# A hybrid decoder step: later weight parts, uncoupled sample scores, more output buffers, and the sample's output inside the last prompt tile

## The chip, the cores and the metric

The kernel runs on one core of a Trainium2 chip. Its engines are TensorE (PE, matrix products, with PEld for the loading of the stationary operand), VectorE (DVE), ScalarE (ACT), GpSimd (POOL) and SyncE (SP, which here issues every DMA). The metric is the device time of one execution in microseconds (us). Three runs of the kernel before gave 1445.16, 1446.93 and 1440.16 us; the median is 1445.16.

## The reference

One inference step of a one-layer decoder: a prompt of 2048 rows and a sample of 8 sequences with 8 new rows each, model width 1024.

```python
h = rmsnorm(x, norm_w)
z = h @ w_in      # q, k, v (512 each), qb, kb (256 each), vb (512), g_lr (16), gate_a, gate_b (512 each)
q = rope(rmsnorm(heads(q, 8), q_norm_w), pos); k = rope(rmsnorm(heads(k, 8), k_norm_w), pos)
o_a = attend(q, k, v)        # mixture of windows (128, step 1), (512, step 4), (2048, step 16)
log_a = log_sigmoid(g_lr @ w_gate_up + b_gate) / 16
o_b, s_fin = gla_chunked(qb / 8, kb, vb, log_a, s0)      # gated linear attention, 4 heads
o_b = rmsnorm(o_b, gla_norm_w)
y = x + concat(o_a * silu(gate_a), o_b * silu(gate_b)) @ w_out
```

The prompt attends within itself. The sample attends to caches of 2048 keys and values per sequence, and its linear attention starts from a given state. All is float32 at the interface; results are y for both, the new keys and values, and the states.

## The kernel before

**Arithmetic and tiles.** The prompt is cut into 16 tiles of 128 rows. A large product is made of three float16 products: an operand is scaled and split into a high and a low part, and high x high, high x low and low x high are summed in PSUM. The weights are cut into blocks of columns (q, k, v, qkb, g, vb, gb and the two halves of the output matrix). `load_w` loads one block as 8 raw tiles, finds its largest magnitude (squares on ACT, for v a reduction on DVE, then `spread_max` on PE), and makes the high and low parts on ACT and DVE. It is a generator: each `yield` lets other work be written in between, and `at_once` runs it to its end. The raw tiles have 8 buffers.

**Prompt rows.** `fetch(t)` loads x of tile t, into one buffer from tile 4 on. `prep(t)` normalises it, splits it, turns it by a transposing DMA (L499) and stores it for later blocks. `project(name, [t])` multiplies tile t by a block (L1056) and `post` takes the result out of PSUM.

**Attention of the prompt.** `attend` (L395 to L450) gives an item four stages: loads; scores on PE (L408), a mask and running minimum on DVE (L416) and exponentials on ACT (L419); transposes of the weights (L426) and their split (L388 to L393, where every second item uses ACT twice and POOL); the product with the values (L441). `pipeline` runs three items staggered by a stage. `unit` serves branches 1 and 2 (64 units, outputs in tile `o` of pool `op`, 4 buffers, stored at L843). `branch3(r)` serves the third branch for residue r of 16: it loads turned queries and keys (L881, L883), copies halves of the queries (`swapped`, L790, L791), loads values (L887), and stores its output tile `o3` (2 buffers of pool `b3`) at L900. The mask instruction writes into the output tile too, so it needs a free one.

**Scores of the sample.** `sample_scores(b, t)` (64 steps, L930 to L946) loads one query row broadcast to all partitions (L935) and cached keys (L937, L940), multiplies on POOL into the single buffer `pr` (L925) and sums on DVE (L926), twice per step. Steps are taken between projections from the third group of tiles on (`dot_next`), and the rest beside block qkb (`dots`).

**Stages.** First v, q, k of tiles 0 to 3; then v, q, k of tiles 4 to 15, with branches 1 and 2 of the tiles before; then block qkb and branch 3; then g, vb and gb with the linear attention; last the output products (`finish`, Y at L1422). Beside these runs the sample's attention, in 4 pairs of sequences: scores, softmax, and 26 value tiles of 8 buffers (`sv`, L1697) multiplied on PE (`OS`, L1671). Each pair ends with DVE's sum `soo` (L1711, L1712), which is stored and read again by `sample_out`, which makes the sample's own rows of y (Y_s).

**Order.** `weave` interleaves generators: always the one with the smallest (steps done + 0.5) / n goes next, so a part with a larger n is served more often. For the last stage the parts are the prompt's output with n = 286 and the sample's attention with n = 64. This gives the order in which instructions are written. The program is built with `schedule_with_timeline_sim=True`: the order on each engine is decided when the program is built, by a planned time at which operands and buffers are ready, and the written order says which goes first. So an instruction can stand far ahead of its place in the text.

## Time and profile before

| quantity | value |
|---|---|
| runs, median (lowest to highest) | 1445.16 us (1440.16 to 1446.93) |
| profiled execution | 1444.89 us |
| its span, first to last instruction | 1443.1 us |
| mean granted TensorE clock | 0.961 |
| PE busy | 89% |
| DVE busy | 70% |
| ACT busy | 59% |
| POOL busy | 43% |
| DMA engines, mean share on the main queue | 67% |

Busy shares are of the span. A line of a timeline gives start, duration, engine, line, operation, output<-input and count, and in brackets how long the engine was idle before it and what ended that. A line of waits gives engine, line and what it waited for, then us in total, times, and the longest. A line of a stretch gives its bounds and length, then busy us of PE, PEld, DVE, ACT and POOL with the number of instructions, the granted clock, the DMA share and GB/s. A line of a source gives minimum/median/maximum duration in ns and the first and last start.

### The profile page before, as it was taken

Reading aid. Unit: us, or ns where it says so; the run is one execution under the profiler, and the core shown is the slowest. Engines: PE = TensorE matmul, PEld = TensorE weight load, DVE = VectorE, ACT = ScalarE, POOL = GpSimd, SP = SyncE. Lnnn points to the kernel's source line nnn. Section 1 sums busy time; section 2 is a strip of 40 time slices with the busy share of each in tenths; the row PEclk is TensorE's granted clock in tenths of the full one; section 3 lists DMA queues with packets and bytes.
Section 4 is the critical chain, followed back from the end, with each engine's and each line's share of the span. In section 5 each row is a group of like instructions: output and inputs, shape, how many; then the busy total and the mean of one; then the engine's idle time right before and its main releaser. Section 6 shows DMA issues by size and latency. Waiting matters only on the chain.

```text
span 1443.1 us, 26500 instructions
## 1 busy us (share of the span) xinstructions
PE 1287.7 (89%) x8878; PEld 741.6 (51%) x8878; DVE 1013.1 (70%) x2445; ACT 853.1 (59%) x2295; POOL 624.8 (43%) x564
## 2 busy tenths in 40 slices
PE   4797998998989799997799999989889979999997
PEld 1343554555546455565466755667545435444343
DVE  6486877888798967667765446899978698773222
ACT  6635677677558866767667764778777543221120
POOL 0052334466667545664420376655752364340000
PEclk9998998999999999999799999999999999999998
DMA  9857585477866798879876453343225769988661
GB/s 280 253 163 181 149 215 145 125 204 224 207 181 190 171 271 260 281 231 245 233 186 161 137 169 103 101 133 119 71 103 192 258 203 339 377 286 267 227 205 62
DMA packets 255194, 285.36 MB, mean 198 GB/s; under 512 B 126209, under 2 KB 157010, under 8 KB 255058
## 3 DMA queue, kind: packets, MB, share of 16 engines
q1 hardware_dynamic: 255058, 283.67, 67.0%
q8 instruction: 70, 1.15, 0.3%
q14 instruction: 66, 0.54, 0.1%
HBM read 183.19 MB, written 75.24 MB: 179 GB/s over the span
## 4 chain that ended last, share of the span: by engine, by line
PE 35%; DVE 22%; DMA 19%; ACT 10%; issue 8%; POOL 4%; SPq 2%; DVEq 0%; POOLq 0%; ACTq 0%
PE Y L1422 8%; DMA T_q<-qp_d 3%; PE acc_vb L1056 3%; PE acc_g L1056 3%; PE OS L1671 3%; DMA x<-in_x_prompt 2%; PE s L408 2%; PE acc_q L1056 2%; PE acc_qkb L1056 2%; DVE p L416 2%; PE acc_v L1056 2%; DVE qbd L221 2%; PE t L426 2%; PE acc_k L1056 2%; ACT p L419 2%
## 5 line engine op out<-in xcount | busy, mean ns | idle before, releaser
L925 POOL TENSOR_TENSOR pr<-k,qb 128x512 f32<-128x512 f32 x128 | 174.8, 1366 | 188.7 <-DVE sck L926 111.7
L1056 PEld LDWEIGHTS <-hr 128*128 128x128 f16 x1824 | 177.6, 100 | 137.7 <-issue 16.5
L419 ACT ACTIVATE p<-p,o 128x256 f32<-128x256 f32 (+1 forms) x384 | 173.2, 453 | 84.3 <-DVE o L416 72.5
L1056 PEld LDWEIGHTS <-hl 128*128 128x128 f16 x1248 | 124.9, 102 | 157.5 <-issue 39.4
L1422 PE MATMUL Y<-w_o,mh 128*128 128x512 f16 x768 | 183.6, 387 | 10.4 <-ACT mh L1388 6.0
L416 DVE CUSTOM_DVE_ANT_0 p<-s,m3w,scl_s 128x256 f32<-128x256 f32 (+1 forms) x384 | 143.4, 418 | 34.4 <-DMA o_d<-o 20.8
L393 POOL TENSOR_TENSOR pt<-p,pt 128x512 f16<-128x512 f32 (+1 forms) x80 | 92.9, 1162 | 139.6 <-ACT pt L392 90.5
L441 PE MATMUL O<-v,pt 128*128 128x128 f16 x1200 | 115.6, 223 | 27.0 <-POOL pt L393 11.4
L426 PE MATMUL t<-ident,p 128*128 128x128 f32 x600 | 117.8, 286 | 14.3 <-ACT p L419 13.2
L1422 PEld LDWEIGHTS <-mh 128*128 128x128 f16 x768 | 72.8, 99 | 106.2 <-issue 27.1
L926 DVE TENSOR_REDUCE sck<-pr 128x8 f32<-128x512 f32 x128 | 87.1, 680 | 56.3 <-POOL pr L925 55.8
L408 PE MATMUL s<-kk,qq 128*128 128x256 f16 (+1 forms) x512 | 107.6, 324 | 17.5 <-DVE o L416 12.6
L1056 PE MATMUL acc_v<-w_v,hl 128*128 128x512 f16 x384 | 101.1, 410 | 13.0 <-ACT zs_k L648 4.6
L441 PEld LDWEIGHTS <-pt 128*128 128x128 f16 x1200 | 85.6, 100 | 51.8 <-POOL pt L393 15.7
L1056 PE MATMUL acc_g<-w_g,hr 128*128 128x272 f16 (+1 forms) x768 | 105.6, 288 | 5.3 <-DVE za L775 3.9
L1056 PE MATMUL acc_q<-w_q,hl 128*128 128x512 f16 x384 | 96.2, 394 | 2.1 <-ACT zs_q L648 1.4
L1056 PE MATMUL acc_k<-w_k,hl 128*128 128x512 f16 x384 | 92.9, 385 | 2.7 <-ACT zs_k L648 2.7
L1388 ACT ACTIVATE mh<-tm 128x1024 f16<-128x1024 f16 x32 | 31.7, 1020 | 104.1 <-PE tm L1387 97.7
L1056 PE MATMUL acc_vb<-w_vb,hr 128*128 128x512 f16 x384 | 91.4, 381 | 1.9 <-DVE so_g L622 1.9
L426 PEld LDWEIGHTS t<-ident,p 128*128 128x128 f32 x600 | 72.0, 145 | 36.0 <-ACT p L419 23.7
L1056 PE MATMUL acc_gb<-w_gb,hr 128*128 128x512 f16 x384 | 88.6, 384 | 0.1
L210 ACT ACTIVATE E<-D_e 128x256 f32<-128x256 f32 (+1 forms) x168 | 67.6, 412 | 31.7 <-DVE ks L217 21.2
(527 smaller groups left out, 2640.2 us busy)
## 6 DMA issues: line engine op xcount, KB each, us to landing
k<-in_cache_k_win SPq DMA_DIRECT2D x104, 256.0 KB, 4.4
sv<-in_cache_v_win SPq DMA_DIRECT2D x104, 256.0 KB, 5.5
hr<-h_d SPq DMA_DIRECT2D x44, 512.0 KB, 4.5
qb<-q_d SPq DMA_DIRECT2D x64, 256.0 KB, 4.7
oc<-o_d SPq DMA_DIRECT2D x48, 264.0 KB, 5.7
o_d<-o SPq DMA_DIRECT2D x64, 132.0 KB, 3.4
x<-in_x_prompt SPq DMA_DIRECT2D x16, 512.0 KB, 5.2
h_d<-hl SPq DMA_DIRECT2D x16, 512.0 KB, 5.1
```

The source lines that it names most:

```text
L210: ACT.activation(E[rows, i, :n], D[rows, half], AF.Exp, scale=1.0 / 16.0)
L393: POOL.tensor_tensor(l, f, h, ALU.subtract)
L408: PE.matmul(s_ps[:, i * w : (i + 1) * w], q, k, start=(n == 0), stop=(n == len(prods) - 1),)
L416: DVE.tensor_tensor_reduce(s[:, sl], s_ps[:, sl], mask, neg, BIG, ALU.add, ALU.min, nmf(i))
L419: ACT.activation(s[:, sl], s[:, sl], AF.Exp, bias=nmf(i), scale=-1.0, accum_out=denf(i))
L426: PE.transpose(p_ps[:, i * P : (i + 1) * P], t["s"][:, i * P : (i + 1) * P], ident[:])
L441: PE.matmul(o_, t["pt"][:, c, (i * nb + b) * P : (i * nb + b + 1) * P], vf(i, b), start=(n == 0), stop=(n == 2 * nb - 1),)
L925: POOL.tensor_tensor(pr[:], kt, qt, ALU.mult)
L926: DVE.tensor_reduce(out, pr[:].rearrange("p (u k d) -> p u k d", u=2, k=4), AX.X, ALU.add)
L1056: PE.matmul(z, a_[:, k, :], w[:, p_, k, cols], start=(k == 0 and i == 0), stop=(k == KT - 1 and i == 2),)
L1422: PE.matmul(Y[:], a_[:, k, :], w_[:, part, k, :512], start=(i == 0), stop=(i == len(prods) - 1),)
L1671: PE.matmul(OS[32 * x : 32 * x + 32, 0:256], ps(x), vs_[bb][:, 256 * u : 256 * u + 256], start=(i == 0), stop=(i == 13),)
```

## The change

- Pool `op` (outputs of branches 1 and 2) has 6 buffers instead of 4, and the float16 parts of k (`kp`) have 2 instead of 1.
- In `branch3` the loads of a residue are written one residue earlier, behind `swapped` of the residue before (`load3`). The values come as two tiles of 512 columns in the 11 buffers of branch 2's values. The output tile `o3` has 3 buffers instead of 2; turned queries and keys keep 2.
- The sample's two products of a step are made in place, into the key tile and into the query tile. The tile `pr` is gone. DVE's two sums, and the store of a finished sequence, are written one step later (`dot_sums`).
- In the first stage the loads of block q, and its first square, are written behind v's tile 0, and the rest of `load_w("q")` behind v's tile 2, followed by the loads of k; the rest of k's stands behind q's tile 1.
- x of a tile is fetched right behind `prep` of the tile before, instead of right ahead of its own `prep`.
- `sample_out` moves from before the last prompt tile to step 8 of that tile's 16 steps (the first step of its second half).
- The pace n of the sample's attention falls from 64 to 52.

```diff
@@ -366,7 +366,7 @@
         xp = right(c_first, "xp", 2)
         sp = c_att.enter_context(tc.tile_pool(name="sp", bufs=3))
         ptp = c_att.enter_context(tc.tile_pool(name="ptp", bufs=3))
-        op = c_att.enter_context(tc.tile_pool(name="op", bufs=4))
+        op = c_att.enter_context(tc.tile_pool(name="op", bufs=6))
         ap_ = c_att.enter_context(tc.tile_pool(name="ap", bufs=2))
         vp = c_att.enter_context(tc.tile_pool(name="vp", bufs=11))
 
@@ -749,7 +749,7 @@
                     ACT.activation(o[:n], o[:n], AF.Copy, scale=unq[:n])
                 SP.dma_start((q_d if nm_ == "q" else k_d)[rows, :], o[:n])
                 return
-            p_ = xp.tile([P, NH, 2, HD], F16, name=f"{nm_}p_{t}", tag=f"{nm_}p", bufs=1)
+            p_ = xp.tile([P, NH, 2, HD], F16, name=f"{nm_}p_{t}", tag=f"{nm_}p", bufs=2 if nm_ == "k" else 1)
             src = o.rearrange("p (h d) -> p h d", h=NH)
             h, l = p_[:, :, 0], p_[:, :, 1]
             if nm_ == "k":
@@ -873,19 +873,33 @@
             return out
 
 
+        T3 = {}
+
+        def load3(r):
+
+            T = T3[r] = {}
+            for nm_, src, shape in (("q", qp_d, [P, 2, NH, P]), ("k", kp_d, [P, 1, NH, P])):
+                t = T[nm_] = b3.tile(shape, F16, name=f"T3_{nm_}_{r}", tag=f"T{nm_}")
+                SP.dma_start_transpose(t[:, 0], by16(src, r))
+            T["v"] = []
+            for i in range(2):
+                v = vp.tile([P, 512], F16, name=f"v3_{r}_{i}", tag="v2", bufs=11)
+                SP.dma_start(v[:], by16(vp_d[:, 512 * i : 512 * i + 512], r))
+                T["v"].append(v)
+
         def branch3(r):
-            T = {}
+            T = T3.setdefault(r, {})
 
             def pre():
-                q = T["q"] = b3.tile([P, 2, NH, P], F16, name=f"T3_q_{r}", tag="Tq")
-                SP.dma_start_transpose(q[:, 0], by16(qp_d, r))
-                k = T["k"] = b3.tile([P, NH, P], F16, name=f"T3_k_{r}", tag="Tk")
-                SP.dma_start_transpose(k[:], by16(kp_d, r))
-                swapped(q)
+                if r == 0:
+                    load3(0)
+                    yield
+                T.update(T3[r])
+                swapped(T["q"])
+                if r < 15:
+                    load3(r + 1)
                 yield
-                T["v"] = b3.tile([P, 1024], F16, name=f"v3_{r}", tag="v3")
-                SP.dma_start(T["v"][:], by16(vp_d[:], r))
-                T["o"] = b3.tile([P, NH, 66], F32, name=f"o3_{r}", tag="o3")
+                T["o"] = b3.tile([P, NH, 66], F32, name=f"o3_{r}", tag="o3", bufs=3)
 
             def OT(a, i):
                 if ("O", a) not in T:
@@ -903,11 +917,11 @@
                 attend(
                     f"3_{r}_{a}", 4, 1,
                     lambda i, a=a: [
-                        (T["q"][:, order_, 2 * i + a], T["k"][:, 2 * i + a])
+                        (T["q"][:, order_, 2 * i + a], T["k"][:, 0, 2 * i + a])
                         for order_ in range(2)
                     ],
                     m3,
-                    lambda i, b, a=a: T["v"][:, (2 * i + a) * P : (2 * i + a + 1) * P],
+                    lambda i, b, a=a: T["v"][i // 2][:, (2 * i + a) % 4 * P :][:, :P],
                     lambda i, a=a: T["o"][:, 2 * i + a, 65:66],
                     lambda i, a=a: T["o"][:, 2 * i + a, 64:65],
                     lambda i, a=a: OT(a, i),
@@ -920,12 +934,16 @@
         q_s = q_d[S : S + NS, :]
         sk_state = {}
 
-        def dot(out, kt, qt, tag):
-            pr = sk.tile([P, 512], F32, name=f"pr_{tag}", tag="pr", bufs=1)
-            POOL.tensor_tensor(pr[:], kt, qt, ALU.mult)
-            DVE.tensor_reduce(
-                out, pr[:].rearrange("p (u k d) -> p u k d", u=2, k=4), AX.X, ALU.add
-            )
+        def dot_sums():
+
+            prods, last = sk_state.pop("sums", ((), None))
+            for out, pr in prods:
+                DVE.tensor_reduce(
+                    out, pr[:].rearrange("p (u k d) -> p u k d", u=2, k=4), AX.X, ALU.add
+                )
+            if last:
+                b, sc = last
+                SP.dma_start(sc_d[b * P : (b + 1) * P, :], sc[:].rearrange("p g c -> p (g c)"))
 
         def sample_scores(b, t):
             if t == 0:
@@ -940,10 +958,12 @@
                 SP.dma_start(k2[:], ck[b, W - 512 : W, :].rearrange("(j r) c -> r j c", r=4)[t])
                 sk_state["k2"] = k2
             out = sc[:].rearrange("p g (u t k) -> p g t u k", u=2, t=8)[:, :, t]
-            dot(out[:, 1], k3[:], qt[:], f"3_{b}_{t}")
-            dot(out[:, 0], sk_state["k2"][:], qt[:], f"2_{b}_{t}")
-            if t == 7:
-                SP.dma_start(sc_d[b * P : (b + 1) * P, :], sc[:].rearrange("p g c -> p (g c)"))
+            dot_sums()
+            POOL.tensor_tensor(k3[:], k3[:], qt[:], ALU.mult)
+            POOL.tensor_tensor(qt[:], sk_state["k2"][:], qt[:], ALU.mult)
+            sk_state["sums"] = (
+                [(out[:, 1], k3), (out[:, 0], qt)], (b, sc) if t == 7 else None
+            )
 
         nwa = kp.tile([P, KT], F32, name="nwa")
         ACT.activation(nwa[:], nw[:], AF.Abs)
@@ -1081,12 +1101,19 @@
                         yield from project(name, [t])
                         if name == "v":
                             if t == 0:
-                                at_once(load_w("q"))
-                            elif t == 3:
-                                at_once(load_w("k"))
+                                w_q = load_w("q")
+                                next(w_q)
+                            elif t == 2:
+                                at_once(w_q)
+                                w_k = load_w("k")
+                                next(w_k)
+                        elif name == "q" and t == 0:
+                            fetch(4)
+                        elif name == "q" and t == 1:
+                            at_once(w_k)
                         elif name == "k":
-                            fetch(t + 4)
                             prep(t + 4)
+                            fetch(t + 5)
                 return
             for t in tiles:
                 for name in "vqk":
@@ -1095,8 +1122,9 @@
                     yield from project(name, [t])
                     dot_next(t)
                 if t < 12:
-                    fetch(t + 4)
                     prep(t + 4)
+                if t < 11:
+                    fetch(t + 5)
             if m == 1:
                 for name in "qk":
                     yield from project(name, ["s"])
@@ -1116,6 +1144,7 @@
                 for b in range(8):
                     for t in (0, 4, 1, 5, 2, 6, 3, 7):
                         side.append(lambda b=b, t=t: sample_scores(b, t))
+                side.append(dot_sums)
         c_first.close()
 
 
@@ -1521,15 +1550,15 @@
         def prompt_out():
             for t in range(NT):
                 rows = slice(t * P, (t + 1) * P)
-                if t == NT - 1:
-                    while "attended" not in mixed:
-                        yield WAIT
-                    yield from sample_out()
                 for i, _ in enumerate(finish(f"{t}", P, mixes.pop(t), x_p[rows, :], y_p[rows, :])):
                     if i == 1 and t + 2 < NT:
                         mixes[t + 2] = combine(t + 2)
                     if i == 2 * KT - 6 and t + 1 < NT:
                         mixes[t + 1] = turned(t + 1, mixes[t + 1])
+                    if t == NT - 1 and i == KT:
+                        while "attended" not in mixed:
+                            yield WAIT
+                        yield from sample_out()
                     yield
 
         weave(host, fetch, [first_mixes(), 2])
@@ -1724,7 +1753,7 @@
                 yield from sample_pair(bp)
             mixed.add("attended")
 
-        weave(out, [sample_attention(), 4 * 16])
+        weave(out, [sample_attention(), 4 * 13])
 
 
 # ---- launch: one core; inputs and outputs as the reference has them ----
```

## The prediction

> **What bounds the kernel now.** I read the first lines of the page, then the busy time by stretch, then who waited for whom, then the timeline at the places that the diff touches.
>
> ```profile
> span 1443.1 us, 26500 instructions
> PE 1287.7 (89%) x8878; PEld 741.6 (51%) x8878; DVE 1013.1 (70%) x2445; ACT 853.1 (59%) x2295; POOL 624.8 (43%) x564
> ```
>
> TensorE (PE) is busy for 1287.7 of 1443.1 us. The edits remove no matrix product, so the time can fall only by what PE stands idle, 155.4 us, or by what runs at a reduced clock. The stretches are: first projections; projections with attention branches 1 and 2 (two rows); their end with the sample scores; branch 3; gated linear attention; output projection.
>
> ```profile
> 0.00:110.00 110.00, 76.88 (x321) 33.32 (x322) 70.04 (x164) 63.09 (x135) 22.11 (x31) 0.97 0.80 231
> 110.00:250.00 140.00, 125.74 (x744) 70.37 (x743) 103.68 (x262) 93.77 (x278) 46.93 (x41) 0.90 0.68 175
> 250.00:505.00 255.00, 225.34 (x1489) 133.37 (x1489) 219.38 (x488) 177.53 (x487) 162.86 (x119) 0.98 0.69 185
> 505.00:690.00 185.00, 166.06 (x1203) 105.91 (x1201) 126.37 (x362) 127.47 (x376) 103.21 (x83) 0.96 0.92 256
> 690.00:830.00 140.00, 127.00 (x1037) 91.30 (x1037) 85.65 (x321) 98.43 (x340) 38.53 (x40) 0.93 0.67 178
> 830.00:1180.00 350.00, 320.25 (x2467) 198.05 (x2466) 279.24 (x586) 240.90 (x601) 193.18 (x208) 0.98 0.45 142
> 1180.00:1443.10 263.10, 246.40 (x1624) 109.28 (x1621) 128.78 (x266) 51.87 (x81) 57.93 (x47) 0.97 0.74 252
> ```
>
> Idle PE time is length minus busy: 33.1, 14.3, 29.7, 18.9, 13.0, 29.8 and 16.7 us. From 250 to 505 VectorE (DVE) is at 219.4 of 255 us, so there a DVE stall costs most.
>
> ```profile
> POOL pr L925 <- DVE sck L926: 111.7, 61, 6.7
> DVE sck L926 <- POOL pr L925: 55.8, 48, 4.3
> DVE T_q L790 <- DMA T_q<-qp_d: 26.6, 12, 5.2
> DVE p L416 <- DMA o_d<-o: 20.8, 11, 3.8
> ...
> PE t L426 <- ACT p L419: 13.2, 11, 4.6
> PE s L408 <- DVE o L416: 12.6, 15, 1.9
> PE O L441 <- POOL pt L393: 11.4, 13, 1.7
> PE O L441 <- DVE pt L389: 6.6, 6, 2.5
> PE O L441 <- DVE o L458: 5.8, 5, 3.3
> ```
>
> DVE stalls for 55.8 us on GpSimd's (POOL's) products, 26.6 us on branch 3's transposed queries and 20.8 us on attention outputs that are still being stored: 103.2 us. PE's named waits on the attention chain are 13.2 + 12.6 + 11.4 + 6.6 + 5.8 = 49.6 us. So one us of these DVE stalls can be worth at most 49.6 / 103.2 = 0.48 us of PE.
>
> **How far order counts.** Engines run in order, but that order is not the program's:
>
> ```profile
> 17.37 0.43 SPq L937 DMA_DIRECT2D k<-in_cache_k_win  x1
> ...
> L925 POOL TENSOR_TENSOR pr<-k,qb x128: 1259/1275/2242, 268.0 to 740.8; 128x512 f32<-128x512 f32 x128
> ```
>
> This cache load belongs to sample step 0, whose product starts at 268.0; it is issued at 17.37. A load goes out as soon as its buffer is free, so an edit that only moves a statement changes a preference, and an edit that changes a buffer or a dependency changes what is possible. I cost the two kinds apart.
>
> **First weights.** Loads of q and k stay early, their squares and parts come later in the program.
>
> ```profile
> 60.56 0.27 PE L536 MATMUL mx_k<-ident,w_k 128*1 128x128 f32 x1 [3.02 <-DVE w_k L579]
> ```
>
> The reduction of k's maxima stands in PE's queue ahead of q's projection and holds it for 3.02 us, waiting for DVE. Moved behind q's tile 1 it finds its input ready. Against it, q's own parts are now asked for at v's tile 2, and late parts would hold q's first product. Bounds: a gain of 3 and a loss of 3 by the same row, since q's reduction would stand where k's stood. I take a gain of 1, nearer to zero because squares can still be placed early.
>
> **Prompt rows one tile earlier.** The load of x is now asked for right behind the preparation that frees its one buffer.
>
> ```profile
> 97.44 1.28 DVE L496 SCALAR_TENSOR_TENSOR ht<-x,rs,ht 128x1024 f16<-128x1024 f32 x1 [0.58 <-ACT ht L495]
> 99.74 2.32 SPq L499 DMA_TRANSPOSE hl<-ht  x1
> 102.95 0.44 SPq L472 DMA_DIRECT2D x<-in_x_prompt  x1
> 108.81 1.06 ACT L487 ACTIVATE jk<-x 128x1024 bf16<-128x1024 f32 x1 [5.57 <-DMA x<-in_x_prompt]
> 111.17 7.82 PE L1056 MATMUL acc_v<-w_v,hl 128*128 128x512 f16 x23 [4.56 <-ACT zs_k L648]
> ```
>
> The buffer is free at 97.44 + 1.28 = 98.72, SP's queue then issues the transposing load until 102.06, and x goes at 102.95. The new place is behind the same transpose, so at most 102.95 - 102.06 = 0.9 us is won per tile. The cost of the lateness is real: ScalarE (ACT) stands 5.57 us on x, and its evacuation behind that holds PE for 4.56 us. I take 0, bounds 0 to a gain of 4.6. A loss is excluded as the load waits for nothing new.
>
> **Branch 3.** Its transposes are asked for one residue ahead, but the tiles keep two buffers.
>
> ```profile
> 726.14 0.50 PE L408 MATMUL s<-T_k,T_q 128*128 128x128 f16 x6
> 728.37 1.35 SPq L881 DMA_TRANSPOSE T_q<-qp_d  x1
> 735.30 0.42 DVE L790 COPY T_q<-T_q 64x1024 f16<-64x1024 f16 x1 [5.18 <-DMA T_q<-qp_d]
> ...
> 755.18 0.35 DVE L416 CUSTOM_DVE_ANT_0 p<-s,m3w,scl_s 128x128 f32<-128x128 f32 x1 [0.65 <-DMA o_d<-o]
> 771.35 0.53 SPq L900 DMA_DIRECT2D o_d<-o  x1
> 774.59 0.35 DVE L416 CUSTOM_DVE_ANT_0 p<-s,m3w,scl_s 128x128 f32<-128x128 f32 x1 [0.32 <-DMA o_d<-o]
> ...
> L900 SPq DMA_DIRECT2D o_d<-o x16: 319/348/1595, 669.0 to 825.0; - x16
> ```
>
> The transpose issued at 728.37 keeps DVE idle for 5.18 us up to 735.30. It goes out as soon as the scores that end at 726.14 + 0.50 have freed its buffer, and the edit leaves that. So 0 for the transposes; the bounds are 0 and all 26.6 x 0.48 = 12.8 us. The third output buffer is another matter. The residue whose first mask stands at 755.18 is stored at 771.35, and the mask of the residue two later ends its wait on that store at 774.59: two residues in 19.4 us, because there are two buffers. The stores' own spacing agrees, (825.0 - 669.0) / 15 = 10.4 us. With three the same life allows 19.4 / 3 = 6.5 us. PE gains little directly, as projections fill that stretch and only 13.0 us are idle; I take 2 us, bounds 0 and 13. Values arrive as two loads instead of one in the eleven buffers of branch 2: 16 more issues of about 0.35 us (the store's row), 5.6 us on SP over the branch, hidden under PE's 127.0 busy us; without that cover they cost 5.6. The second buffer for k's parts I take as 0, bounds 0 and 1, since no large wait names it.
>
> **Output buffers 4 to 6, and the sample's products.** The 20.8 us of DVE waits on stores should go. The products no longer share one buffer: POOL makes both of a step in place, and DVE sums them one step later. POOL's 111.7 us of waits on DVE's sums lose their cause. Of DVE's 55.8 us I count half, 27.9, because the sum can still be placed where its product is due by plan and be late again when a cache load lands late. So 48.7 us of stalls go, at most 48.7 x 0.48 = 23.4 us of PE. I take 10, below half, as ACT's exponentials lie between DVE and PE. Bounds: 0, and 76.6 x 0.48 = 36.8 with all of both.
>
> The change adds a wait: the loads of queries and keys now wait for DVE's sum of two steps before, not for POOL's product.
>
> ```profile
> SPq L937 <- POOL pr L925: 36.8, 31, 4.1
> ```
>
> At the key load SP already stands 36.8 us, with attention stores and branch-3 loads queued behind it, for which DVE and PE wait in turn. Two more output buffers absorb a late store, and POOL's products come sooner without their own waits. I take 0; bounds: the 36.8 us vanish, or they double, 36.8 x 0.48 = 17.7 us either way.
>
> **The end.** The sample's output moves from before the last prompt tile into its middle.
>
> ```profile
> 1412.52 3.63 PE L1422 MATMUL Y_s<-w_o,mh_s 128*128 128x512 f16 x16
> 1413.04 0.60 DVE L1711 TENSOR_REDUCE soo<-so 128x64 f32<-128x256 f32 x1
> 1420.45 0.64 PE L1399 MATMUL mt_s<-ident,mix_s 64*128 64x64 f32 x4 [4.30 <-DVE mix_s L1500]
> 1422.03 6.25 PE L1422 MATMUL Y_s<-w_o,mh_s 128*128 128x512 f16 x16 [0.94 <-DVE mh_s L1405]
> 1428.11 10.52 PE L1422 MATMUL Y<-w_o,mh 128*128 128x512 f16 x48
> ...
> L1712 DVE TENSOR_SCALAR soo<-soo,sml x4: 250/254/255, 1268.9 to 1413.7; 128x64 f32<-128x64 f32 x4
> ```
>
> Sixteen products take 3.63 us, then PE waits 4.30 and 0.94 us for the last attention values, which leave at 1413.04 and come back through memory. The next sixteen take 6.25 us, 2.6 more. Gap and slow products cost 4.3 + 0.9 + 2.6 = 7.8 us. The last tile's 48 products (10.52 us) stand behind; in the new order at least 27 of them stand in front, 27/48 x 10.52 = 5.9 us, and 21 more are ready beside. They cover the 9.0 us from 1413.04 to 1422.03 only if the values end no later. The pace number falls from 64 to 52, and a smaller number is served less often, so the values are asked for more slowly. By the 64, the pairs' 44 steps are due within 44/64 x 286 = 197 output steps, in tile 12; the last ends at 1413.7, when tile 15 alone is left. They seem held by their loads, which a smaller number doesn't slow. I take 5; bounds: a gain of 7.8 and the loss of the third rival.
>
> [...]
>
> **Sum.** 1 + 0 + 2 + 10 + 5 = 18 us. The profiled execution took 1444.89 us, its span and 1.8 us around it; 1444.9 - 18 = **1427 us**. The median of the runs is 1445.16, so the same gain stands against it.
>
> **Rivals.**
> - Order only: the plan places the sums and transposes where they were, and late landings keep DVE as late. For it speaks the load at 17.37, against it the shared buffers that really go. Left are 1 + 5: 1439.
> - Everything: all 76.6 us of DVE stalls convert at 0.48, and the end gains 5: 1444.9 - 36.8 - 5 = 1403. Against it speak the 26.6 us on transposes, which stay in the same queue.
> - Slower: the sample's values now follow their lower pace. Pairs end 1268.9 to 1413.7, three spacings of 48.3 us. Stretched by 64/52, they end 33.4 us later, at 1447. Then come 8.3 us to 1422.03's place, 6.25 us of products and the 4.5 us from the last product (1428.11 + 10.52) to the end: 1466.1 + 1.8 = 1467.9, less 13 won before: 1455. It decides once the last values end after the last tile's own products. For it speaks that the first pair was late from the start; against it, DMA at 0.74 in this stretch.
> - POOL beside DVE: products that no longer pause run more beside DVE's two-input work. A product takes 1275 ns in the median and up to 2242; 64 such add 62 us on POOL, and the 11.4 us that PE waits for POOL double: 1444.9 + 11.4 - 6 = 1450. [...]
>
> **How the numbers follow.** Chances: forecast 0.52, order only 0.22, everything 0.10, slower pace 0.12, POOL 0.04. Half a per cent, 7.2 us, is about what can be told from no change here: faster means under 1437.9, slower over 1452.4. Faster: 0.50 + 0.02 + 0.10 = 0.62; the same: 0.02 + 0.20 + 0.02 = 0.24; slower: 0.12 + 0.02 = 0.14. The forecast's own range is 1414 to 1438 (the middle terms at about 20 and 3). The range reaches into the order-only and POOL cases and down towards the full conversion, and up to where slower begins, which also holds the doubled wait of SP (1427 + 17.7 = 1445): 1405 to 1452, leaving out the slower case and half of the full conversion, 0.17.
>
> **What would show it.** DVE's wait for POOL's product falls to about half of 55.8 and its wait for stores to near 0; POOL's wait for sums nearly vanishes. Branch 3's stores come less than 9 us apart. The wait for transposes stays over 15 us, and x still leaves about 3 us behind its buffer. No PE gap over 2 us stands ahead of the sample's output products. If PE's waits on the attention chain stay near 49.6 us although the DVE stalls go, my 0.48 is no cause; if the last values end after the last tile's products, the pace was the mistake.

## The result, and the profile after

The changed kernel takes 1485.63 us in the median of four runs (1480.58 to 1489.57), the kernel before 1442.84 us beside it: a ratio of 1.0292, interval 1.0248 to 1.0337. It is **slower by 2.9%**. 1427 us, the range up to 1452 us and the sign were all wrong.

First the busy times on the page of the kernel after, then its busy times by stretch, in the prediction's columns and with bounds at 270 and 505 us:

```profile
span 1487.6 us, 26552 instructions
...
PE 1292.8 (87%) x8878; PEld 743.8 (50%) x8878; DVE 1016.8 (68%) x2445; ACT 850.8 (57%) x2295; POOL 622.6 (42%) x564
```
```profile
110.00:270.00 160.00, 135.42 (x846) 77.63 (x847) 116.45 (x293) 106.08 (x312) 52.46 (x48) 0.94 0.68 176
270.00:505.00 235.00, 195.92 (x1230) 112.05 (x1228) 193.47 (x402) 141.38 (x386) 158.72 (x116) 0.96 0.72 193
505.00:690.00 185.00, 155.29 (x1027) 96.10 (x1027) 131.69 (x327) 117.22 (x327) 113.27 (x88) 0.92 0.82 238
690.00:830.00 140.00, 122.29 (x1110) 92.27 (x1109) 93.27 (x394) 117.34 (x423) 24.00 (x23) 0.94 0.70 173
```

The same stretches of the kernel before, where they were not shown:

```profile
110.00:270.00 160.00, 142.43 (x835) 79.90 (x835) 117.77 (x293) 105.44 (x310) 52.59 (x46) 0.89 0.63 165
270.00:505.00 235.00, 208.65 (x1398) 123.84 (x1397) 205.30 (x458) 165.87 (x454) 157.20 (x114) 0.99 0.72 192
```

PE's busy time is that of before (1292.8 to 1287.7 us), so the 44.5 us longer span is nearly all idle time, 194.8 instead of 155.4 us. To see where it arises, I multiply PE's busy time by the granted clock, as a rough measure of matrix work done. From 270 to 690 us the kernel before does 208.65 x 0.99 + 166.06 x 0.96 = 366 us of it, the kernel after 195.92 x 0.96 + 155.29 x 0.92 = 331 us. That is 35 us lost in this stretch, of which 23.5 are more idle time and the rest a lower clock there (over the whole span the mean clock is nearly that of before, 0.958 to 0.961). Most of the loss therefore lies beside the sample's scores, and little of it at the start, in branch 3 or at the end.

Who waits for whom in the kernel after (totals, times, longest):

```profile
POOL k L962 <- DMA qb<-q_d: 52.6, 19, 9.9
DVE sck L941 <- POOL k L962: 49.6, 34, 6.1
...
DVE sck L941 <- POOL qb L963: 31.9, 19, 5.5
...
PE O L441 <- POOL pt L393: 29.3, 20, 3.1
...
POOL qb L963 <- DMA k<-in_cache_k_win: 28.1, 12, 6.3
...
DVE T_q L790 <- DMA T_q<-qp_d: 18.8, 10, 3.6
...
DVE p L416 <- DMA o_d<-o: 9.5, 4, 4.1
```

The same view for SP's own queue:

```profile
SPq L955 <- DVE sck L941: 46.1, 31, 6.2
...
SPq L953 <- DVE sck L941: 29.7, 20, 7.1
```

POOL's 111.7 us of waits on sums are nearly gone (7.6 us), as meant. But DVE's waits on products rose from 55.8 to 49.6 + 31.9 = 81.5 us, and POOL now waits 52.6 + 28.1 us for loads in the lines above and 8.6 us in a third, 89.3 us. PE's wait for POOL's evictions `pt` (attention's turned weights) rose from 11.4 to 29.3 us. Between 270 and 690 us, all waits of PE in this view add up to 67.4 us instead of 42.9, and 17.0 of these 24.5 us are on `pt` (27.2 instead of 10.2). And the sums ended earlier, not later; the sums of the kernel before, then of the kernel after (first and last start):

```profile
L926 DVE TENSOR_REDUCE sck<-pr x128: 664/681/690, 269.3 to 742.1; 128x8 f32<-128x512 f32 x128
```
```profile
L941 DVE TENSOR_REDUCE sck<-k x64: 662/685/689, 271.4 to 689.9; 128x8 f32<-128x512 f32 x64
L941 DVE TENSOR_REDUCE sck<-qb x64: 669/679/687, 274.3 to 690.8; 128x8 f32<-128x512 f32 x64
```

The last sum starts at 690.8 instead of 742.1 us. In return DVE starts 180 instead of 215 of attention's 384 masks (L416) between 270 and 690 us. As a mark of the order I take the 113th of the 128 sums: 288 masks stood ahead of it on DVE before, 236 now. Without the shared product buffer, the planner placed the score steps ahead of attention's work.

### The profile page after: what moved, and what is told of

Same layout as the page of the kernel before. It is cut to its first block, busy times and chain, and to the rows that moved or that the text cites. A ratio compares the mean times of both kernels' runs of the same rounds, so it can differ in the third digit from the quotient of the medians.

```text
span 1487.6 us, 26552 instructions
## 1 busy us (share of the span) xinstructions
PE 1292.8 (87%) x8878; PEld 743.8 (50%) x8878; DVE 1016.8 (68%) x2445; ACT 850.8 (57%) x2295; POOL 622.6 (42%) x564
## 4 chain that ended last, share of the span: by engine, by line
PE 28%; DVE 23%; DMA 16%; ACT 6%; issue 5%; POOL 4%; SPq 2%; POOLq 0%; DVEq 0%; ACTq 0%
PE Y L1451 9%; DMA k<-in_cache_k_win 5%; PE OS L1700 3%; PE acc_vb L1076 3%; DVE p L416 3%; PE acc_g L1076 2%; DMA qb<-q_d 2%; DVE sck L941 2%; POOL qb L963 2%; DVE qbd L221 1%; PE acc_qkb L1076 1%; POOL k L962 1%; DMA T_q<-qp_d 1%; PE acc_gb L1076 1%; DVE ks L217 1%
## 5 line engine op out<-in xcount | busy, mean ns | idle before, releaser
L419 ACT ACTIVATE p<-p,o 128x256 f32<-128x256 f32 (+1 forms) x384 | 173.1, 454 | 111.7 <-DVE o L416 103.0
L1451 PE MATMUL Y<-w_o,mh 128*128 128x512 f16 x768 | 187.6, 387 | 9.0 <-ACT mh L1417 4.7
L441 PE MATMUL O<-v,pt 128*128 128x128 f16 x1200 | 119.2, 229 | 48.7 <-POOL pt L393 29.3
L416 DVE CUSTOM_DVE_ANT_0 p<-s,m3w,scl_s 128x256 f32<-128x256 f32 (+1 forms) x384 | 143.8, 419 | 18.6 <-DMA o_d<-o 9.5
L962 POOL TENSOR_TENSOR k<-k,qb 128x512 f32<-128x512 f32 x64 | 87.0, 1361 | 108.9 <-DMA qb<-q_d 52.6
L426 PE MATMUL t<-ident,p 128*128 128x128 f32 x600 | 113.4, 291 | 16.3 <-ACT p L419 14.1
L1076 PE MATMUL acc_v<-w_v,hl 128*128 128x512 f16 x384 | 100.2, 411 | 19.1 <-ACT zs_k L648 10.9
L1076 PE MATMUL acc_g<-w_g,hr 128*128 128x272 f16 (+1 forms) x768 | 99.3, 279 | 2.6 <-ACT vbs L722 2.6
L963 POOL TENSOR_TENSOR qb<-k,qb 128x512 f32<-128x512 f32 x64 | 86.3, 1350 | 36.3 <-DMA k<-in_cache_k_win 28.1
L1076 PE MATMUL acc_q<-w_q,hl 128*128 128x512 f16 x384 | 91.5, 387 | 1.5 <-DVE vp L735 1.5
```

The costliest lines, as they stand in the source:

```text
L416: DVE.tensor_tensor_reduce(s[:, sl], s_ps[:, sl], mask, neg, BIG, ALU.add, ALU.min, nmf(i))
L419: ACT.activation(s[:, sl], s[:, sl], AF.Exp, bias=nmf(i), scale=-1.0, accum_out=denf(i))
L426: PE.transpose(p_ps[:, i * P : (i + 1) * P], t["s"][:, i * P : (i + 1) * P], ident[:])
L441: PE.matmul(o_, t["pt"][:, c, (i * nb + b) * P : (i * nb + b + 1) * P], vf(i, b), start=(n == 0), stop=(n == 2 * nb - 1),)
L962: POOL.tensor_tensor(k3[:], k3[:], qt[:], ALU.mult)
L963: POOL.tensor_tensor(qt[:], sk_state["k2"][:], qt[:], ALU.mult)
```

## The experiments

Eighteen runs. Times are medians; the kernel before took 1444.3 to 1446.9 us beside them. Columns 2 and 3 of this table are read from each trace between 270 and 740 us: POOL's waits for the loads of queries and keys, and PE's products waiting for POOL's `pt`. Column 4 is the number of masks ahead of DVE's 113th score sum. The expectations count "output adds" there; these are all of the trace's records of L416, which besides a mask hold its readout and waits in the queue (672 for the 288 masks of the kernel before). Column 5 is the start of tile 9's v projection, beside which the first products of the scores run (us).

| run | POOL on loads | PE on `pt` | masks ahead | v of tile 9 | time (us) |
|---|---|---|---|---|---|
| before | 34.8 | 10.2 | 288 | 270 | 1442.84 |
| after | 89.3 | 28.6 | 236 | 269 | 1485.63 |
| all but the score edit | 60.1 | 11.9 | 288 | 271 | 1447.41 |
| score edit alone | 83.6 | 22.2 | 238 | 270 | 1486.61 |
| start alone | 35.3 | 3.1 | 296 | 271 | 1449.13 |
| end alone | 57.3 | 10.6 | 288 | 270 | 1446.38 |
| in place, sums at once | 90.9 | 22.9 | 236 | 269 | 1491.77 |
| in place, three tiles each | 84.5 | 18.3 | 218 | 259 | 1467.17 |
| two product buffers | 59.2 | 18.9 | 228 | 268 | 1472.09 |
| the same, sums late | 59.4 | 18.5 | 228 | 268 | 1478.68 |
| in place, one key tile | 103.1 | 31.3 | 272 | 256 | 1476.20 |
| two product buffers, one load tile each | 168.0 | 37.7 | 280 | 257 | 1503.20 |
| branch 3 alone | 34.3 | 8.0 | 300 | 268 | 1452.57 |
| before, one query tile | 104.5 | 22.0 | 336 | 269 | 1510.26 |
| no loads, one product buffer | 0 | 1.1 | 296 | 259 | 1415.08 |
| no loads, two product buffers | 0 | 1.3 | 214 | 258 | 1422.26 |
| branch 3, three key tiles | 38.7 | 3.6 | 304 | 259 | 1439.22 |
| unread loads, one product buffer | 0 | 0.5 | 296 | 258 | 1498.22 |
| unread loads, two product buffers | 0 | 0 | 216 | 256 | 1489.86 |
| branch 3, start, end, three key tiles | 69.1 | 11.0 | 288 | 268 | 1466.58 |

### Which part costs

All edits but the one of the sample's scores (k's parts keep one buffer: the tile `pr` stays, with the 2 KB a partition that a second would take):

```diff
-            dot_sums()
-            POOL.tensor_tensor(k3[:], k3[:], qt[:], ALU.mult)
-            POOL.tensor_tensor(qt[:], sk_state["k2"][:], qt[:], ALU.mult)
+            dot(out[:, 1], k3[:], qt[:], f"3_{b}_{t}")
+            dot(out[:, 0], sk_state["k2"][:], qt[:], f"2_{b}_{t}")
```

> All of the change but the sample's scores, which stay as before (one product buffer, two sums at once; k's parts keep one buffer, since the memory does not hold both). Theory: the held key and query tiles of the scores cost the whole loss, so this gives about 1440 us (1430 to 1447). Rival: the loss comes from the first weights and the changed order (ten us are lost before tile 4 already) or from the other buffers; then it stays over 1470.

1447.41 us, ratio 1.0006 (0.9987 to 1.0025): no change, where the prediction's other terms add up to a gain of 8 us. Then the score edit alone, in the kernel before:

```diff
-            dot(out[:, 1], k3[:], qt[:], f"3_{b}_{t}")
-            dot(out[:, 0], sk_state["k2"][:], qt[:], f"2_{b}_{t}")
+            dot_sums()
+            POOL.tensor_tensor(k3[:], k3[:], qt[:], ALU.mult)
+            POOL.tensor_tensor(qt[:], sk_state["k2"][:], qt[:], ALU.mult)
```

> The kernel before with the sample's in-place products and later sums alone. Theory of the held tiles: 1475 to 1490 us, with attention outputs late from the third group of tiles on and POOL waiting over 45 us on query loads. Rival (loss from elsewhere): 1437 to 1448.

1486.61 us, ratio 1.0289 (1.0255 to 1.0323), the whole loss. Its two stretches from 270 to 690 us hold 200.37 x 0.93 + 160.45 x 0.91 = 332 us of work, as in the kernel after, though with less of it idle time: over the whole span PE is busy for 1303.9 us instead of 1287.7 with the same products, so 16 of the 44 us are slower products (mean granted clock 0.941 instead of 0.961).

```profile
270.00:505.00 235.00, 200.37 (x1240) 114.74 (x1238) 189.17 (x395) 139.94 (x383) 149.49 (x112) 0.93 0.69 186
505.00:690.00 185.00, 160.45 (x1058) 98.52 (x1059) 131.46 (x331) 120.94 (x336) 116.06 (x90) 0.91 0.86 247
```

The start's edits alone (loads, squares and parts of q and k later, x one tile earlier):

```diff
-                                at_once(load_w("q"))
-                            elif t == 3:
-                                at_once(load_w("k"))
...
+                        elif name == "q" and t == 1:
+                            at_once(w_k)
```

> The kernel before with the later weight parts and the earlier fetch of x alone. The changed kernel is 10 us late at the first product of v's tile 4. Theory: these 10 us are made up behind, since by tile 9 the changed kernel stood level: 1440 to 1450 us. Rival: they stay: 1450 to 1457.

1449.13 us, ratio 1.0025 (1.0004 to 1.0046): no gain, at most a small loss. Tile 4's first v product starts at 121.9 instead of 111.2 us, tile 9's at 270.6 instead of 269.6: ten us are lost ahead of tile 4 and made up by tile 9. The end's edits alone:

```diff
-        weave(out, [sample_attention(), 4 * 16])
+        weave(out, [sample_attention(), 52])     # and sample_out amid the last tile
```

> The kernel before with the sample's output inside the last tile and the pace of 52 alone. Theory: the gap ahead of the sample's output products is partly closed and the values end later, 3 to 5 us won at the end, 1438 to 1442 us. Rival of the slower pace: 1447 or more.

1446.38 us, ratio 1.0020 (1.0003 to 1.0037). The timeline of this run's end shows why nothing came of it:

```profile
1427.50 0.25 DVE L1712 TENSOR_SCALAR soo<-soo,sml 128x64 f32<-128x64 f32 x1
...
1429.54 1.89 PE L1422 MATMUL Y_s<-w_o,mh_s 128*128 128x512 f16 x8
...
1431.27 0.59 PE L1422 MATMUL Y<-w_o,mh 128*128 128x512 f16 x2
...
1433.88 5.34 PE L1422 MATMUL Y_s<-w_o,mh_s 128*128 128x512 f16 x24
```

The last values leave at 1427.5 us, against 1413.7 before. The sample's output products run late and last, to 1433.88 + 5.34 = 1439.2 us, where before the prompt's own ended at 1438.6 us.

### Held tiles or late sums

In place and one step late, a product holds its load tile longer. First the sums written in the same step:

```diff
             sk_state["sums"] = (...)
+            dot_sums()
```

> The kernel before with products in place, but DVE's two sums written right behind them, in the same step. Held tiles (query and key tiles, two buffers each, now come free with DVE's sum instead of POOL's product): still clearly slow, 1455 to 1490 us. Late sums (it is the step's delay that costs): 1437 to 1450 us.

1491.77 us, ratio 1.0332 (1.0304 to 1.0359). Sums at once bring nothing. Then the three tiles of each kind:

```diff
-            qt = sk.tile(..., tag="qbc")
+            qt = sk.tile(..., tag="qbc", bufs=3)      # and k3 likewise; branch 3's edits make room
```

> The kernel before with branch 3's edits (for the memory) and the sample's edit as changed, but three query and three key tiles instead of two. Held tiles: the third buffer pays for the longer hold, 1435 to 1450 us, and POOL's wait on query loads falls under 30 us. Late sums or products too eager: 1470 to 1490 us.

1467.17 us, ratio 1.0149 (1.0130 to 1.0168). It recovers some 20 us, but POOL's waits for loads did not fall as expected (84.5 us, 83.6 with two tiles), and not all of the 20 us need be the tiles': tile 9's v projection starts at 259 instead of 270 us here, ahead of the first sum. The runs fall into two groups by this column, 256 to 259 and 268 to 271 us: a changed buffer makes the plan anew also where nothing was edited. Comparisons between the two groups can hold up to some 10 us of this; how much of such a lead lasts to the end is not shown. Next, products go into two buffers of their own, so that POOL is uncoupled and no load tile is held; sums at once, and then a step later:

```diff
-            pr = sk.tile(..., tag="pr", bufs=1)
+            pr = sk.tile(..., tag="pr", bufs=2)       # branch 3's edits make room
```

> Branch 3's edits, and the scores as before but with two product buffers instead of one: POOL is uncoupled and no load tile is held. Held tiles: 1430 to 1446 us, DVE's wait on products below 45 us. If uncoupling itself costs (products taken too eagerly, beside attention): 1455 or more.

> As the run with two product buffers, but DVE's sums written one step later, as in the change. Held tiles: 1430 to 1450 us, since the load tiles still come free with the product. Late sums: 1465 to 1490 us.

1472.09 us, ratio 1.0188 (1.0169 to 1.0207), and 1478.68 us, ratio 1.0233 (1.0218 to 1.0249). Late sums cost 6.6 us. But a second product buffer, with no load tile held, already costs 19.5 us over branch 3 alone (1452.57 us, below). Held tiles are not the whole cause; uncoupling itself costs.

### Order or late loads

The score steps' place in the order can be moved by the number of load tiles. One key tile with the score edit, then one tile of each kind with two product buffers:

```diff
-            k3 = sk.tile(..., tag="k3")
+            k3 = sk.tile(..., tag="k3", bufs=1)
```

> The kernel before with the sample edit alone (products in place, sums one step late), and the rotating key tile k3 cut from two buffers to one. Read so far: with the sums uncoupled, the planner puts the score steps further forward in the engines' orders; in the trace of the kernel before, 672 of attention's output adds stand on DVE ahead of the 113th score sum, with the edit alone 567. With one key tile the next step's key load must wait for the sum of the step before, so the loads are held longer still, but the planned order comes back near that of before (some 650 adds ahead of the 113th sum). Held-load theory: slower than the edit alone, 1490 us or more, with POOL's waits for loads above the 62 + 18 us of the edit alone (270 to 700 us). Order theory: most of the loss goes away though the loads are held longer, 1445 to 1460 us, and PE's busy time at the granted clock between 270 and 690 us comes back from 332 us to 355 or more (before: 367).

```diff
-            pr = sk.tile(..., tag="pr", bufs=1)
+            pr = sk.tile(..., tag="pr", bufs=2)       # branch 3's edits make room
-            qt = sk.tile(..., tag="qbc")
+            qt = sk.tile(..., tag="qbc", bufs=1)      # and k3 likewise
```

> As the run with two product buffers and the sums at once (branch 3's edits, products into their own two tiles; it took 1472 us), with one query tile and one key tile instead of two each. POOL and DVE stay uncoupled; the single load tiles spread the steps, so that the planned order is about that of before (some 660 adds ahead of the 113th sum, against 537 with two load tiles). Order theory: 1440 to 1455 us. A theory in which the uncoupling itself costs (DVE's sums or POOL's products at a bad moment, whatever their place): 1470 us or more.

1476.20 us, ratio 1.0215 (1.0198 to 1.0232), and 1503.20 us, ratio 1.0404 (1.0381 to 1.0427). They put the sums back to 272 and 280 masks. The first is 10 us faster than the score edit alone, though POOL waits longer for loads; the held-load theory had it slower, and the order theory had it at 1460 us or less. As tile 9 starts 14 us earlier in it, the 10 us needn't be the order's. PE's work between 270 and 690 us does come back, to 201.17 x 0.97 + 159.64 x 1.00 = 355 us, as the order theory had it; the time does not. The second is 31 us slower than with two load tiles, where the order theory had it at 1455 us or less: an order like that of before does not help where loads are late. The waits of the second run, from 270 to 740 us:

```profile
POOL pr L939 <- DMA qb<-q_d: 153.3, 38, 8.3
DVE sck L940 <- POOL pr L939: 116.2, 63, 5.5
...
PE O L441 <- POOL pt L393: 37.7, 21, 4.7
```

On POOL attention's `pt` stand behind these 153.3 us of waits for queries, and PE waits 37.7 us for them. Next the control, branch 3's edits alone:

```diff
+                if r < 15:
+                    load3(r + 1)
...
-                T["o"] = b3.tile([P, NH, 66], F32, name=f"o3_{r}", tag="o3")
+                T["o"] = b3.tile([P, NH, 66], F32, name=f"o3_{r}", tag="o3", bufs=3)
```

> The kernel before with branch 3's edits alone (next unit's loads at the start of a unit, values in two halves, third output buffer); the control for the runs that build on them. Score steps as before. All theories: branch-3 units at about 8 us instead of 10.5, and a time of 1436 to 1446 us; the sum of the prediction gave it 2 us. If it is 1455 or more, the loss of the runs with two product buffers is not the uncoupling's.

1452.57 us, ratio 1.0056 (1.0035 to 1.0078), above the 1436 to 1446 us that every theory had. Then the reverse of the displacement, in the kernel before:

```diff
-            qt = sk.tile(..., tag="qbc")
+            qt = sk.tile(..., tag="qbc", bufs=1)
```

> The kernel before, nothing else changed, with one query tile for the score steps instead of two. The steps then stand further back in the order than before (some 750 of 768 adds ahead of the 113th sum on DVE). Order theory in its simplest form, the later the better: 1430 to 1443 us. If the order has a best place near that of before, because the steps left over then hold up branch 3 and the inputs of the gated recurrence: 1447 to 1470 us. Held-load theory: slower, 1450 us or more, with POOL's waits for query loads well above the 25 us of before.

1510.26 us, ratio 1.0451 (1.0433 to 1.0470). "The later the better" fell. Single query tiles alone turn 34.8 us of waits for loads into 104.5 and cost 66 us.

### Uncoupled, with nothing to wait for

Loads left out but for the first of each kind, with one and with two product buffers:

```diff
-            qt = sk.tile(..., tag="qbc")
-            SP.dma_start(qt[:], ...)
+            if "q" not in sk_state:
+                qt = sk_state["q"] = sk.tile(..., tag="qbc", bufs=1)
+                SP.dma_start(qt[:], ...)               # k3 and k2 likewise
```

> The kernel before, with the score steps' loads left out but for the first of each kind (one query row, one key tile of each branch): all 128 products read the same tiles, so the scores are not the sample's; the products, the sums and one product buffer stay. 157 loads of 256 KB and every wait of POOL for them are gone. Base for the run beside it. Late-load theory: below before by part of the 35 us of POOL's load waits and of the lighter queues, 1415 to 1440 us. Order theory: the order on DVE is about that of before, so a time near before's, 1430 to 1445 us.

```diff
-            pr = sk.tile(..., tag="pr", bufs=1)
+            pr = sk.tile(..., tag="pr", bufs=2)
```

> As the run without sample loads, with two product buffers instead of one, so that POOL is uncoupled from DVE's sums and nothing of the score steps can wait for a load. The planner puts the steps further forward than in any run so far (some 500 output adds ahead of the 113th sum on DVE, against 672 in the kernel before). Late-load theory: no slower than the run with one product buffer, a difference of -15 to +5 us. Order theory: slower by 20 to 45 us, as with the loads, and PE's busy time at the granted clock between 270 and 690 us falls by 15 us or more.

1415.08 and 1422.26 us. The second buffer costs 7.2 us here, although the sums are moved further forward than in any run with loads (214 masks). The waits from 270 to 740 us with one, then with two product buffers:

```profile
POOL pr L925 <- DVE sck L926: 139.2, 78, 5.7
...
DVE sck L926 <- POOL pr L925: 24.3, 31, 1.7
...
PE O L441 <- POOL pt L393: 1.1, 2, 0.7
```
```profile
POOL pr L925 <- DVE sck L926: 55.2, 42, 3.8
...
DVE sck L926 <- POOL pr L925: 9.5, 11, 1.4
...
PE O L441 <- POOL pt L393: 1.3, 3, 0.8
```

This is what the prediction had in mind, POOL and DVE both freed (139.2 to 55.2 and 24.3 to 9.5 us), and even this wins nothing. If costs carry over from one kernel to the other, the displaced order explains some 7 of the 19.5 us that a second product buffer cost with loads, and the other 12 or so need the loads; that is an estimate from two pairs of runs. A third key tile in the coupled form:

```diff
-            k3 = sk.tile(..., tag="k3")
+            k3 = sk.tile(..., tag="k3", bufs=3)        # with branch 3's edits
```

> Branch 3's edits alone (1452.6 us), with three key tiles for the score steps instead of two; products and sums coupled by one buffer as before. Each key load can start one step earlier. POOL's 27 us of waits for key loads should fall below 10. Late-load theory: 1438 to 1448 us, faster than branch 3's edits alone by 5 to 14 us. Order theory: the order stays that of before, 1448 to 1456 us.

1439.22 us, ratio 0.9949 (0.9930 to 0.9968): a little faster than the kernel before, by 0.5%. The number expected came for another reason than expected. POOL's waits for key loads, with two key tiles and then with three, did not fall:

```profile
POOL pr L939 <- DMA k<-in_cache_k_win: 27.1, 9, 4.4
```
```profile
POOL pr L939 <- DMA k<-in_cache_k_win: 31.1, 14, 4.3
```

27.1 and 31.1 us. What differs stands ahead of the scores: tile 9's v projection, the first beside them, starts at 259 instead of 268 us, the other group of plans. So this run is no evidence on late loads. Then loads as traffic only, into two rotating tiles that nothing reads, with one and with two product buffers:

```diff
+            qt = k3 = sk_state["k2"] = sk_state["q"]    # one resident tile
+            un = sk.tile(..., tag="un")                 # two buffers
+            SP.dma_start(un[:], ...)                    # each former load
```

> The kernel before, with all 160 score loads issued as before (same sources, 256 KB each), but into two rotating tiles that nothing reads; all products read one resident tile, so the scores are not the sample's. One product buffer. Base for the run beside it. If the waits for loads cost and the traffic does not: near the pair's base without loads, 1412 to 1425 us. If the traffic costs: 1430 to 1445 us.

```diff
-            pr = sk.tile(..., tag="pr", bufs=1)
+            pr = sk.tile(..., tag="pr", bufs=2)
```

> As the run with unread loads, with two product buffers. Traffic is there, the score steps are placed some 500 output adds deep at the 113th sum, and no product can wait for a load. Waits theory: slower than its base by 0 to 10 us, as in the pair without loads (7). Traffic theory: slower by 15 to 30 us, as with loads that are read (20 between branch 3's edits with one and with two product buffers).

1498.22 and 1489.86 us. The second buffer gains 8.4 us here, where one theory had it at a loss of 0 to 10 us and the other at 15 to 30, and no product ever waits for a load. So what a second buffer costs depends on the kernel around it. Both are 68 to 83 us slower than without loads, more than any theory allowed, and 44 to 52 us slower than the kernel before, which issues the same loads. The waits of the first, 270 to 740 us, and those of SP's queue:

```profile
DVE p L416 <- DMA o_d<-o: 70.4, 10, 16.9
...
PE s L408 <- DVE o L416: 43.6, 11, 15.6
```
```profile
SPq L941 <- DMA un_k<-in_cache_k_win: 66.7, 48, 3.4
SPq L944 <- DMA un_q<-q_d: 44.0, 26, 2.6
```

SP stands these 66.7 and 44.0 us until an earlier load has landed, so that its tile may be written again, and attention's stores stand behind it in its queue: DVE waits 70.4 us for them, where the kernel before waits 10.9 us in this time. Last, the third key tile beside branch 3's, the start's and the end's edits:

```diff
-            k3 = sk.tile(..., tag="k3")
+            k3 = sk.tile(..., tag="k3", bufs=3)        # with those edits
```

> Branch 3's edits, the start's and the end's, four output buffers, the score steps as in the kernel before but with three key tiles. From the runs alone: 1439 us (branch 3 with three key tiles) + 4 (start) + 2 (end) = 1445 us if they add up. If the edits help each other as they seemed to where all but the score edit were made (1447 us for parts that add up to 1459): 1430 to 1438 us.

1466.58 us, ratio 1.0135 (1.0105 to 1.0165). The start's and the end's edits cost 4.5 and 1.8 us alone and 27 us here; tile 9 starts at 268 us again, 9 us later than without them. The rest is not explained.

## Why the prediction was wrong, point by point

- **The sample's products: the step that failed.** "I take 10" for products without a shared buffer; measured alone, the edit costs 42 us. Two thoughts in it were wrong. DVE's wait for products should halve to 27.9 us; it rose to 81.5, because POOL, no longer paced by the sums, ran up to its loads. And the shared buffer was read as a stall only. It was also what kept the score steps back in the plan: a second one moves them from 300 to 228 masks with loads, from 296 to 214 without. POOL's 111.7 us of waits on sums held up little that PE needed (11.4 us on `pt`); its 89.3 us on loads did (29.3 us). Perhaps this is because the plan counts the former and not the lateness of a landing; that is argued, not shown. Without loads DVE's wait for products does fall when POOL is uncoupled (24.3 to 9.5 us), so its rise here needs the loads.
- **The factor 0.48.** A microsecond of DVE stall was priced by PE's waits. In the kernel after the three DVE stalls did not go (81.5 + 18.8 + 9.5 = 109.8 us, 103.2 before), so it could not show there. In the pair without loads DVE's stall falls by 14.8 us and the time rises by 7.2. The factor has no support here.
- **"The change adds a wait ... I take 0."** SP's wait at the key loads rose from 36.8 to 46.1 us only, inside the bounds. The effect was on who waits for the loads: POOL, with attention's evictions behind it. The prediction named the work behind SP, not the work behind POOL. The unread loads, where SP waits for landings, cost 44 to 52 us over the kernel before, more than the 17.7 us bound.
- **Branch 3.** The mechanism held: the 16 stores are now (832.7 - 716.7) / 15 = 7.7 us apart, below the 9 named.

```profile
L914 SPq DMA_DIRECT2D o_d<-o x16: 319/324/571, 716.7 to 832.7; - x16
```

  Its term did not: 2 us forecast (0 to 13), measured alone a loss of 8.3 us. There branch 3's last scores start 22 us earlier than before (785 instead of 807 us), and block gb's last product, of the linear attention, ends 10 us later (1167 instead of 1158). Why is not settled.
- **Output buffers.** The waits for stores fell from 20.8 to 9.5 us, not to near 0. Those on the stores of branches 1 and 2, which got the buffers, went from 17.6 us to none, as forecast; the 9.5 us are on branch 3's, 3.3 us before. The transposes' wait stayed above 15 us, at 18.8, as foreseen.
- **First weights and x.** The 3.02 us hold at k's reduction went away, and its place was taken by k's parts, which hold k's first product for 3.69 us:

```profile
79.06 0.27 PE L536 MATMUL mx_k<-ident,w_k 128*1 128x128 f32 x1
...
84.79 1.01 PE L1076 MATMUL acc_k<-w_k,hl 128*128 128x512 f16 x2 [3.69 <-ACT w_k L603]
```

  That is about the bound of a loss of 3, named and not taken; the prediction looked for it at q's first product, and it came at k's. The load of x still leaves 3.1 us behind its buffer (113.09 against 108.75 + 1.27), as said:

```profile
108.75 1.27 DVE L496 SCALAR_TENSOR_TENSOR ht<-x,rs,ht 128x1024 f16<-128x1024 f32 x1
...
113.09 0.43 SPq L472 DMA_DIRECT2D x<-in_x_prompt  x1
```

  But "a loss is excluded" was wrong. x's buffer is itself freed 11.3 us later than before, and the wait that the prediction priced at 4.56 us, that of tile 4's first v product for ACT behind x, has grown:

```profile
118.49 1.06 ACT L487 ACTIVATE jk<-x 128x1024 bf16<-128x1024 f32 x1 [3.93 <-DMA x<-in_x_prompt]
...
120.84 4.54 PE L1076 MATMUL acc_v<-w_v,hl 128*128 128x512 f16 x14 [10.91 <-ACT zs_k L648]
```

  With the start's edits alone it is 11.62 us. By tile 9 this is made up; these edits alone take 4.5 us more in all (1449.13 to 1444.58), by the interval 0.6 to 6.6. Weights and x were not run apart, so which of the two delays x stays open.
- **The end.** Its term was 5; measured a loss of 1.8 us. The third rival's mechanism is what happened, at less than half of its size: values 14 us later instead of 33. They still leave ahead of the prompt's own last products (1427.5 to 1431.27 us), but the sample's output products now come last. The gap ahead of these shrank as forecast, from 4.30 to 1.45 us with the end alone.
- **The rivals.** POOL beside DVE falls: a product takes 1361 and 1350 ns on average in its two lines, 1366 before. The seven longest of before (2183 to 2242 ns) do all run beside DVE's L684, so something is shown of what this rival supposes; but after there are no more of them, six of 2241 to 2262 ns, beside L683 or L684. "Order only" took the plan to leave the sums where they were; they moved, and forward. Slower had a chance of 0.14, none of it for the steps being planned too early or for late loads.

What stays open: how the 12 to 13 us that need the loads divide between POOL's waits for them and their place in SP's queue. The sum of POOL's waits is not enough by itself: the runs with all but the score edit and with the end alone show about 60 us of it, as the two product buffers do, and lose next to nothing. Their steps stand at 288 masks, as before. Early steps and late loads came together in the five runs that lost 22 to 47 us with the sums uncoupled and two or three load tiles, and in the changed kernel. The runs with single load tiles or unread loads lost 32 to 66 us by longer waits, all but one of them with 272 masks ahead or more, and the last run's 20 us are not explained.

## What to carry to other kernels

Where a planner places the work, a shared buffer can also be a brake (here a second one moved the score steps from 300 to 228 masks): before it is removed, ask what will then run earlier, in which engine's queue it will wait for its loads, and whose work stands behind it. Test an edit of a dependency alone, since edits that each cost or gain some microseconds don't add up once the plan is made anew: here the parts alone lose 42, 8, 5 and 2 us, and all together 43 (the output buffers and k's second part buffer were not run alone). An engine's total wait was no price here (111.7 us of POOL's waits on sums stood beside 11.4 us of PE's on `pt`, 89.3 us of waits on loads beside 29.3); look for the wait at which TensorE ends up.

## What the runs showed of the hardware that was not expected

- A wait of SP at one load showed as a wait of DVE for stores that SP issues. With 160 loads that nothing reads and one product buffer, SP stood 66.7 and 44.0 us at two of the loads for earlier landings, DVE's wait for attention's stores rose from 10.9 to 70.4 us, and the time was 52 us above the kernel before with the same loads. The DMA engines' mean share from 270 to 740 us was 0.75, below the 0.81 of the kernel before, so a fuller DMA does not explain it.
- The granted clock was lower where the score edit cost time: 0.99 and 0.96 in the two stretches from 270 us before, 0.96 and 0.92 after, 0.93 and 0.91 with the score edit alone. In the kernel after this is a third of the work lost in these stretches. Gaps on TensorE alone do not explain it: from 110 to 270 us the kernel before has 0.89 with PE busy for 142.43 of 160 us, the kernel after 0.94 with 135.42. What sets the clock stays open.
